# Reversed query tiles, the gated unit begun beside the last projection products, and w_out loaded in two halves

## The chip, the cores and the metric

The kernel runs on one core of a Trainium2 chip. The core's engines are TensorE (PE in the profile; PEld is its weight load), VectorE (DVE), ScalarE (ACT), GpSimd (POOL) and SyncE (SP), which issues most transfers. They run beside each other and wait for each other by semaphores. The metric is the device time of one execution in microseconds; lower is better. Before the change the median of three runs is 2513.12 us (2510.8 to 2517.88).

## The reference

One layer of a hybrid decoder over 2048 rows of width 1024, in float32 (`qa`, `ka`, `va`, `qc`, `kvc` are column blocks of `proj`, the queries and keys normed per head of 64):

```python
h = rms_norm(x, norm1_g[l])
proj = jnp.einsum('bld,de->ble', h, w_in[l])
o_a = swa_sink_mixer(qa, ka, va, sinks[l], rel_bias[:, :SWA_HEADS])
o_b = s5_mixer(proj[..., OFF_U:OFF_QC], ssm_a_re[l], ..., glu_w[l], glu_b[l])
gc = jax.nn.sigmoid(proj[..., OFF_GC:IN_WIDTH].reshape(Bsz, L, NSA_HEADS, NSA_BRANCHES))
o_c = nsa_mixer(qc, kvc, gc, cmp_pos[l], ..., rel_bias[:, SWA_HEADS:])
mixed = jnp.concatenate([rms_norm(o_a, ...), rms_norm(o_b, ...), rms_norm(o_c, ...)], axis=-1)
x = x + jnp.einsum('ble,ed->bld', mixed, w_out[l])
h2 = rms_norm(x, norm2_g[l])
hid = jax.nn.relu(jnp.einsum('bld,df->blf', h2, w_up[l]))
x = x + jnp.einsum('blf,fd->bld', hid * hid, w_down[l])
```

`swa_sink_mixer` is attention in a window of 128 with 4 query heads on 2 key heads, a learned sink per head and a bias by distance. `s5_mixer` is a complex diagonal state-space scan, then a GELU and a gated linear unit: `ab = z @ glu_w + glu_b`, the first half times the sigmoid of the second. `nsa_mixer` has 4 heads and three branches (compressed blocks, selected blocks, a window of 512), added with the 12 gates `gc` of a row. In both attentions the bias of a score depends on the distance between query and key alone:

```python
lg = jnp.where(valid, lg + bias, NEG_INF)          # bias = bias_tbl[rel_bucket(i - j + 128)]
```

## The kernel before, in words

Rows are worked in 16 tiles of 128. A float32 product is made of three matmuls (`mm3`, L76 to L78): operands are split into a high part (a cast on ACT) and a low part (a difference on DVE), and high x high, low x high and high x low are added in PSUM.

The phases, by the profile's time: `phase_front` (0 to 407 us) makes the projections in column chunks a, b, c, u, v, one product a chunk and tile, each in two half-products of 12 matmuls; beside them it computes the state-space tables and, in `ssm_steps`, the 16 pair-steps of the scan. Projections go to DRAM (`pa`, `pb`, `pc`), by stores on ACT's queue and SP's. Then (407 to about 560) the window attention (`swa_steps`), the first 11 tiles of the gated unit (`glu_steps`), the bias tables (`bias_steps`) and the block compression (`compress_steps`). `phase_mix` (to about 1240) is the sparse attention, tile by tile, with the rest of the gated unit and then the w_out products (`finish_steps`) as fillers. `phase_up` and `phase_down` are the feed-forward part.

What sets the order: `merge` interleaves lists of steps evenly by their counts, and a tile scheduler orders each engine's instructions by the written order and by priorities (the gated unit's and w_out's products have a lower one, so they fill gaps). Each engine runs its instructions in that order. SP issues its transfers in order too; they go round over eight lanes that it shares with ACT's stores, and a transfer waits for the one before it on its lane.

Three places matter here.

*The front's end.* `merge(rest[:-4], ssm_steps(...)) + rest[-4:]`: of 49 steps of the last projection chunks, 45 are merged with the state-space steps, and the last 4 half-products (L77 to L78, `pm_c`) follow alone. Then come the gated unit's first turned tile (L656, `gpt`, from `z` in SBUF), its split (L659, L660), and 13 matmuls for a half-product (`gpm`). Its weights are loaded and split by L635 to L637 (`graw`, `glu_h`, `glu_l`).

*The bias tables.* A table row per query is the same vector shifted by one. The kernel before loads it so that the partition p holds the vector from p on (`T`, 128 x 2033, for each of four heads, L736; `Ts` for the window attention), which is the table with its queries in reverse. Matmuls with the reversed identity `c_anti` (`flip`, L721) turn it over in PSUM, and ACT copies the result (L722) into `b_sel`, `b_cmp`, `b_swa`. The vector itself is made in the front by `bias_vectors` (matmul L704, copy L706, store to `r2`).

*The opening of w_out.* At tile `OPEN` = 2 of `phase_mix`, when the gated unit is done and its memory is free, `open_late` computes the norm factors of the first two mixers (`r_a`, `r_c`, by a Newton iteration of small DVE operations, L44 to L54), and `load_wout` loads the eight 128-row pieces of w_out (L1097, 512 KB each) and splits both halves of each (L1099 on ACT, L1100 on DVE). Then `finish_steps` of tile 0 turns its mixed rows (L1257, `ptx`), splits them (L1260) and makes 8 products for each half of the output columns (`pw`). The raw pieces and the residual tile `mx` share two buffers (tag "xt").

The gates of a tile are made in `prep` (tanh L1123, DVE L1124), from 12 columns that its row load brings along. Queries are turned by `turn` (L835), keys by the same.

Of the kernel before, what the change touches and what calls it, by code (L numbers as in the profile page):

```python
# [80 lines left out]
def phase_front(tc, C, x, xt_in, norm1_g, w_in, u_st, pd, rh_a, prm, dkp, dca, pre, extra, done):  # L81

    nc = tc.nc
    with ExitStack() as ctx:
# [170 lines left out]
        tp = ctx.enter_context(tc.tile_pool(name="sg", bufs=2))  # L255
# [3 lines left out]
        run(merge(rest[:-4], ssm_steps(tc, C, S, u_st, dkp, dca, tp, ps_g, ps_t)) + rest[-4:])  # L259
# [360 lines left out]
def glu_steps(tc, C, ctx, z_st, glu_w, glu_b, ob, ss, ps_x):  # L620
# [4 lines left out]
    ps = ctx.enter_context(tc.tile_pool(name="g_ps", bufs=1, space=PSUM, side="right", reuse_waits="tile"))  # L625
    wh = wp.tile([P, 4, 1024], F32R, name="glu_h")
# [65 lines left out]
def bias_vectors(tc, tp, ps, rel_bias, oh2, ohs, r2, rs):  # L692
# [5 lines left out]
    for src, dst, n in ((oh2, r2, 432), (ohs, rs, 384)):  # L698
        for j in range(src.shape[1] // n):
# [7 lines left out]
            nc.sync.dma_start(dst[:, sl], rv[:, 0:n])  # L707


def bias_steps(tc, C, B, pool, tp, ps, rel_bias, r2, rs):  # L710
# [8 lines left out]
    def flip(n, src, dst, name):  # L719
        pf = ps.tile([P, 512], F32, tag="pg", name="bpf" + name)  # L720
        nc.tensor.matmul(pf[:, 0:n], C["anti"], src, start=True, stop=True)  # L721
        nc.scalar.copy(dst, pf[:, 0:n])  # L722

    def swa(h):
        if h == 0:
            B["Ts"] = tp.tile([P, 4, 256], F32, tag="Ts", name="Ts")
            base = rs[0]
            nc.sync.dma_start(B["Ts"], bass.AP(base.tensor, base.offset, [[1, P], [384, 4], [1, 256]]))
        flip(512, B["Ts"][:, h:h + 2], B["swa"][:, h:h + 2], f"s{h}")
# [102 lines left out]
def turn(nc, C, pool, qd, h0, n, name):  # L832
    pt = pool.tile([P, 4, P], F32, tag="pt", name="pt" + name, bufs=1)
    for j in range(n):
        nc.tensor.transpose(pt[:, j], qd[:, h0 + j].rearrange("p a d -> p (a d)"), C["ident"])  # L835
# [117 lines left out]
def swa_steps(tc, C, ctx, sinks, gains, bias, pd, oa_d, ps, ss, rh):  # L953
# [14 lines left out]
    def prep(i):  # L968
# [5 lines left out]
        pt = turn(nc, C, ps_t, qd, 0, 4, f"qa{i}")  # L974
# [58 lines left out]
def phase_mix(tc, C, x, gains, B, cmp, w_out, out_norm_g, g2, pd, oa_d, ob, x1, hT, xs, rr, rh, ss_a, ss_b, r_d, rest, release):  # L1033
    nc = tc.nc
    kcA, kcB, vc = cmp
    with ExitStack() as ctx:
# [25 lines left out]
        late = {}  # L1062

        def open_late():
# [13 lines left out]
            ra, rc = (fp.tile([P, NT], F32, name=n) for n in ("r_a", "r_c"))  # L1078
            rsqrt_into(nc, sm, ra, ss_a, 1.0 / 256, NT, "ra")
# [892 lines left out]
```

## Time and profile before

| | |
|---|---|
| median of three runs | 2513.12 us |
| the profiled execution | 2511.36 us, span 2509.6 us |
| PE busy | 2428.8 us (97%) |
| DVE, ACT, POOL busy | 1754.9 us (70%), 1325.4 us (53%), 1118.8 us (45%) |
| mean granted clock of PE | 0.989 |
| flips and their copies | 14 flips on PE (28 matmuls, two for each), 14 copies on ACT |
| transfers | 328.82 MB, mean 131 GB/s |

Busy times are sums over an engine's instructions; matmuls overlap each other, so the time that a matmul adds is seen from its start to the next one's. The granted clock is a factor on PE's speed: at 0.50 the same matmuls take twice as long, and PE still shows as busy. A line of waits reads: engine, what waited, `<-` what ended the wait, then the sum, the number and the longest of the waits. A row of the windows has, after the stretch and its length, the busy time (and count) of PE, PEld, DVE, ACT and POOL, then the clock, the busy share of the DMA engines and their GB/s.

### The profile page before, as it was taken

The numbers are of one execution on the slowest core, as the hardware profiler recorded it, in microseconds if no ns is written. First come the engines' busy times: TensorE is split into PE (matmuls) and PEld (weight loads), VectorE is DVE, ScalarE is ACT, GpSimd is POOL, SyncE is SP. The second block draws the span as 40 slices with busy tenths as digits, with TensorE's granted clock in tenths as the row PEclk, the third lists the DMA queues.
The fourth block names the chain that finished last, engine by engine and source line by source line (L and its number), as shares of the span: only waits on it lengthen the run. The fifth ranks groups of instructions, "written<-read, shape, count | busy, mean of one in ns | idle before, by whom it ended". The sixth has DMA issues, their size and how long they took to land. (4 is left out here: it accounts for less than half of the span.)

```text
span 2509.6 us, 38157 instructions
## 1 busy us (share of the span) xinstructions
PE 2428.8 (97%) x12712; PEld 2051.5 (82%) x12712; DVE 1754.9 (70%) x3653; ACT 1325.4 (53%) x2767; POOL 1118.8 (45%) x1034
## 2 busy tenths in 40 slices
PE   8999999999999999999999999999999999999999
PEld 8999997787788778888788877788887888888887
DVE  4775885866688787887464455755556988888886
ACT  6354555765576665665465555555444444334442
POOL 3011222223244444454566666665654435445447
PEclk9999999999999999999999999999999999999999
DMA  5174325311221211222677666755547543444436
GB/s 178 63 211 127 114 90 170 96 56 50 67 75 47 68 47 62 79 89 81 210 213 203 190 191 186 230 163 147 149 131 261 155 124 101 135 135 127 126 100 197
DMA packets 398325, 328.82 MB, mean 131 GB/s; under 512 B 52102, under 2 KB 364044, under 8 KB 396304
## 3 DMA queue, kind: packets, MB, share of 16 engines
q1 hardware_dynamic: 360880, 299.59, 40.1%
q10 hardware_dynamic: 37248, 26.80, 3.4%
q8 instruction: 100, 1.64, 0.3%
q14 instruction: 97, 0.79, 0.1%
HBM read 213.86 MB, written 112.45 MB: 130 GB/s over the span
## 5 line engine op out<-in xcount | busy, mean ns | idle before, releaser
L1429 ACT CAST v<-vr 128x512 fp32r<-128x512 f32 x224 | 139.6, 624 | 296.0 <-DMA vr<-vd 109.1
L1429 DVE TENSOR_TENSOR v<-vr,v 128x512 fp32r<-128x512 f32 x224 | 232.2, 1044 | 78.0 <-ACT v L1429 77.7
L1767 PE MATMUL pdb<-dw,v 128*128 128x512 f32 x768 | 186.3, 392 | 2.0 <-DVE v L1429 2.0
L1767 PE MATMUL pdc<-dw,v 128*128 128x512 f32 x768 | 184.9, 389 | 2.3 <-ACT dw L1429 1.6
L1767 PE MATMUL pda<-dw,v 128*128 128x512 f32 x768 | 184.5, 389 | 0.0
L1545 POOL TENSOR_TENSOR fs<-ur,ur 128x512 f32<-128x512 f32 x64 | 94.1, 1471 | 181.1 <-DMA ur<-in_w_up 100.5
L1767 PEld LDWEIGHTS pdb<-dw,v 128*128 128x128 f32 x768 | 145.1, 189 | 32.5 <-DVE v L1429 2.4
L1429 DVE TENSOR_TENSOR ul<-ur,uh 128x512 fp32r<-128x512 f32 x96 | 91.1, 950 | 114.3 <-ACT uh L1429 114.3
L1767 PEld LDWEIGHTS pdc<-dw,v 128*128 128x128 f32 x768 | 144.0, 188 | 32.9 <-ACT dw L1429 2.0
L1767 PEld LDWEIGHTS pda<-dw,v 128*128 128x128 f32 x768 | 144.4, 188 | 30.1
L1429 ACT CAST uh<-fs 128x512 fp32r<-128x512 f32 x128 | 78.3, 621 | 144.3 <-PE pub L1574 57.1
L1429 DVE TENSOR_TENSOR ul<-fs,uh 128x512 fp32r<-128x512 f32 x128 | 131.6, 1031 | 32.3 <-ACT uh L1429 32.2
L896 POOL TENSOR_SCALAR sls<-sls,dens,gt 128x128 f32<-128x128 f32 (+15 forms) x64 | 80.4, 1257 | 124.5 <-DVE dens L895 91.9
L913 DVE TENSOR_TENSOR tls<-pps,ths 128x512 fp32r<-128x512 f32 (+1 forms) x144 | 93.8, 657 | 33.2 <-ACT ths L912 28.1
L912 ACT CAST ths<-pps 128x512 fp32r<-128x512 f32 (+1 forms) x144 | 79.8, 561 | 67.2 <-PE poc L920 53.4
L76 PE MATMUL pw<-wo_h,mh 128*128 128x512 f32 x256 | 109.2, 427 | 4.2 <-ACT mh L1259 2.0
L1574 PE MATMUL pub<-fh,uh 128*128 128x512 f32 x256 | 103.2, 403 | 4.0 <-DVE e L1583 4.0
L78 PE MATMUL pw<-wo_h,ml 128*128 128x512 f32 x256 | 104.6, 409 | 1.4 <-DVE ml L1260 1.4
L77 PE MATMUL pw<-wo_l,mh 128*128 128x512 f32 x256 | 105.5, 412 | 0.0
L896 POOL TENSOR_SCALAR slw<-slw,denw,gt 128x640 f32<-128x640 f32 (+4 forms) x64 | 53.2, 832 | 116.1 <-DVE denw L895 90.6
L1590 POOL TENSOR_TENSOR ev<-e,e 128x512 f32<-128x512 f32 x64 | 92.2, 1441 | 27.0 <-ACT e L1587 16.4
L1574 PE MATMUL puc<-fh,uh 128*128 128x512 f32 x256 | 100.9, 395 | 3.1 <-DVE eu L1583 3.1
(564 smaller groups left out, 7906.1 us busy)
## 6 DMA issues: line engine op xcount, KB each, us to landing
vr<-vd SPq DMA_DIRECT2D x224, 256.0 KB
ur<-in_w_up SPq DMA_DIRECT2D x128, 256.0 KB
vd<-ev SPq DMA_DIRECT2D x128, 256.0 KB
vd<-e ACTq DMA_DIRECT2D x64, 256.0 KB
dr<-in_w_down SPq DMA_DIRECT2D x32, 512.0 KB
x<-in_x SPq DMA_DIRECT2D x16, 512.0 KB
mx<-in_x SPq DMA_DIRECT2D x16, 512.0 KB
x<-mx ACTq DMA_DIRECT2D x16, 512.0 KB
```

The source lines that it names most:

```text
L76: nc.tensor.matmul(out, sh, mh, start=first, stop=False)
L77: nc.tensor.matmul(out, sh, ml, start=False, stop=False)
L78: nc.tensor.matmul(out, sl, mh, start=False, stop=last)
L896: nc.gpsimd.tensor_scalar(x, x, den[:, h:h + 1], gate, op0=ALU.mult, op1=ALU.mult)
L912: nc.scalar.copy(th[:, 0:nb], pt[:, 0:nb])
L913: nc.vector.tensor_tensor(tl[:, 0:nb], pt[:, 0:nb], th[:, 0:nb], op=ALU.subtract)
L1429: return (nc.scalar.copy(dh, src), nc.vector.tensor_tensor(dl, src, dh, op=ALU.subtract))
L1545: nc.gpsimd.tensor_tensor(t, x, y, op=op)
L1574: nc.tensor.matmul(bank[b], w[:, k], h[o][:, k], start=first and k == 0 and n == 0, stop=k == HALF - 1 and n == 2, skip_group_check=True)
L1590: nc.gpsimd.tensor_tensor(tile_("v" + o), x, y, op=op)
L1767: nc.tensor.matmul(bank[b, q], x[:, q, j], y[:, j], start=first and j == 0 and n == 0, stop=j == 1 and n == 2, skip_group_check=True)
```

## The change

1. Queries stand reversed in each tile of both attentions: `turn` of the queries uses `c_anti` in place of the identity, and where the mixed rows are turned for w_out, chunks 0, 1, 6 and 7 (window and sparse attention) are turned back the same way. The bias tables are loaded from DRAM already in that order, and `flip` with its copies is gone. For the compressed branch, which takes every 16th element, `bias_vectors` writes the vector also as `rc`, 8 x 16 x 135, five copies and five stores more.
2. The gates of all tiles come from one load, one flip, one tanh and one DVE operation (`gate_steps`).
3. The state-space steps are merged with 41 of the 49 steps; beside the last 8 half-products stand the first 13 steps of the gated unit (all weights and biases, three turned tiles, both half-products of tile 0); `open_glu` returns them.
4. `r_a` is computed at the beginning of `phase_mix`. `load_wout(k, n)` loads and splits one half of a piece; the first halves stand where the loads stood, the second ones between the products of tile 0's first half.

```diff
+LAST = 8
+GLU_AHEAD = 13
...
-        run(merge(rest[:-4], ssm_steps(tc, C, S, u_st, dkp, dca, tp, ps_g, ps_t)) + rest[-4:])
+        run(merge(rest[:-LAST], ssm_steps(tc, C, S, u_st, dkp, dca, tp, ps_g, ps_t)))
+        c_s.close()
+        run(merge(rest[-LAST:], open_glu()))
...
             nc.scalar.copy(rv[:, 0:n], pr[0:8, 0:n])
             nc.sync.dma_start(dst[:, sl], rv[:, 0:n])
+            if dst is r2:
+                rd = tp.tile([8, 16, 27], F32, tag="b_rd", name=f"brd{j}")
+                nc.scalar.copy(rd, pr[0:8, 0:n].rearrange("p (c r) -> p r c", r=16))
+                nc.sync.dma_start(rc[:, :, 27 * j:27 * j + 27], rd)
...
-    def flip(n, src, dst, name):
-        pf = ps.tile([P, 512], F32, tag="pg", name="bpf" + name)
-        nc.tensor.matmul(pf[:, 0:n], C["anti"], src, start=True, stop=True)
-        nc.scalar.copy(dst, pf[:, 0:n])
...
-        T = tp.tile([P, 2033], F32, tag="T", name=f"T{h}")
         base = r2[4 + h]
-        nc.sync.dma_start(T, bass.AP(base.tensor, base.offset, [[1, P], [1, 2033]]))
-        for j in range(2):
-            flip(512, T[:, 993 + 512 * j:993 + 512 * j + 512], B["sel"][:, h, 512 * j:512 * j + 512], f"{h}{j}")
-        flip(P, T[:, 0:2033:16], B["cmp"][:, h], f"c{h}")
+        nc.sync.dma_start(B["sel"][:, h], bass.AP(base.tensor, base.offset + 993, [[1, P], [1, 1024]]))
+        base = rc[4 + h]
+        nc.sync.dma_start(B["cmp"][:, h], bass.AP(base.tensor, base.offset, [[1, 8], [135, 16], [1, P]]))
...
+def gate_steps(tc, C, gt, tp, ps, src):
...
+        nc.sync.dma_start(box["g"], src.rearrange("(i p) c -> p i c", p=P)[:, :, 384:396])
...
+        nc.tensor.matmul(pf, C["anti"], box["g"].rearrange("p i c -> p (i c)"), start=True, stop=True)
+        nc.scalar.activation(flat, pf, AF.Tanh, scale=0.5)
+        nc.vector.tensor_scalar(flat, flat, 0.5, 0.5, op0=ALU.mult, op1=ALU.add)
...
-        nc.tensor.transpose(pt[:, j], qd[:, h0 + j].rearrange("p a d -> p (a d)"), C["ident"])
+        nc.tensor.transpose(pt[:, j], qd[:, h0 + j].rearrange("p a d -> p (a d)"), C[order])
...
-        def load_wout(k):
+        def load_wout(k, n):
             fp, wh, wl, go = (late[n] for n in ("fp", "wh", "wl", "go"))
-            for n in range(2):
...
+            sl = slice(512 * n, 512 * n + 512)
+            raw = fp.tile([P, D], F32, tag="xt", name=f"oraw{k}_{n}", bufs=2)[:, 0:512]
+            nc.sync.dma_start(raw, w_out[0, k * P:(k + 1) * P, sl])
+            nc.scalar.activation(wh[k][:, sl], raw, AF.Copy, scale=go[:, k:k + 1])
+            nc.vector.scalar_tensor_tensor(wl[k][:, sl], raw, go[:, k:k + 1], wh[k][:, sl], op0=ALU.mult, op1=ALU.subtract)
...
-                    nc.tensor.transpose(pt[:, j], box["mix"][:, k * P:(k + 1) * P], C["ident"])
+                    nc.tensor.transpose(pt[:, j], box["mix"][:, k * P:(k + 1) * P], C["ident" if 2 <= k < 6 else "anti"])
...
-            res = [load, lambda: turned(0, 4), lambda: turned(4, 8)] + [lambda n=n, k=k: filler(n, k) for n, k in order]
+            res = [load, lambda: turned(0, 4), lambda: turned(4, 8)] + [lambda n=n, k=k: ((load_wout(k, 1) if i == 0 and n == 0 else None), filler(n, k)) for n, k in order]
...
-                    queue += [lambda k=k: load_wout(k) for k in range(NK)]
+                    queue += [lambda k=k: load_wout(k, 0) for k in range(NK)]
...
-            run(merge(swa, glu[:cut], b_nsa + c_steps + [lambda: None] * 6))
+            run(merge(swa, glu[GLU_AHEAD:cut], b_nsa + gs[:1] + c_steps[:6] + gs[1:] + c_steps[6:] + [lambda: None] * 4))
```

What this moves on PE at the front's end. Before, the last projection matmul (`pm_c`) is followed by the gated unit's first turned tile, the flips and its first half-product (`gpm`), and the first query tile (`ptqa`):

```order
L77 MATMUL pm_c_4812<-wl_c_7_4324,hh_2432 128x396
L78 MATMUL pm_c_4812<-wh_c_7_4323,hl_2433 128x396
L656 MATMUL gpt_5024<-c_ident,z_5022 128x128 x4
L721 MATMUL bpfs_4923<-Ts,c_anti 128x512
L656 MATMUL gpt_5412<-c_ident,z_5410 128x128 x2
L721 MATMUL bpfs_4926<-Ts,c_anti 128x512
L656 MATMUL gpt_5412<-c_ident,z_5410 128x128 x2
L721 MATMUL bpf_4998<-T_4996,c_anti 128x512
L76 MATMUL gpm_5449<-glu_h,zh_5029 128x512
```

Now the second turned tile stands before the last product (`pm_c_4928`), the first in the middle of the first of the four, and half-products follow the last one directly:

```order
L664 MATMUL gpt_4903<-c_ident,z_4901 128x128 x4
L76 MATMUL pm_c_4928<-wh_c_0_4177,hh_2448 128x396
...
L78 MATMUL pm_c_4928<-wh_c_7_4407,hl_2449 128x396
L76 MATMUL gpm_4912<-glu_h,zh_4778 128x512
L77 MATMUL gpm_4912<-glu_l,zh_4778 128x512
...
L76 MATMUL gpm_4941<-glu_h,zh_4778 128x512
L664 MATMUL gpt_4979<-c_ident,z_4977 128x128 x4
L854 MATMUL ptqa_5054<-c_anti,qda_5052 128x128 x4
```

The turned tile and its split no longer stand between the last product and the first half-product, and no flip does.

On PE after the opening, where tile 0's products (`pw`) begin; before, they begin when its rows are turned (`ptx`), ahead of the probabilities' turns `ppw` of that tile:

```order
L1257 MATMUL ptx_8467<-c_ident,mix_8409 128x128 x4
L920 MATMUL poc_8510<-tls_8808,Vs 128x256 x2
...
L76 MATMUL pw_8483<-wo_h_8103,mh_8430 128x512
L77 MATMUL pw_8483<-wo_l_8104,mh_8430 128x512
L78 MATMUL pw_8483<-wo_h_8103,ml_8431 128x512
...
L909 MATMUL ppw_8921<-c_ident,slw_8695 128x128
```

Now `ppw_8902`, the same turns, stand ahead of the second `ptx`, and two further groups of them before the first product:

```order
L928 MATMUL ppw_8902<-c_ident,slw_8676 128x128
...
L1271 MATMUL ptx_8419<-c_ident,mix_8361 128x128 x2
L1271 MATMUL ptx_8419<-c_anti,mix_8361 128x128 x2
...
L928 MATMUL ppw_9002<-c_ident,slw_8797 128x128
L76 MATMUL pw_8439<-wo_h_8091,mh_8382 128x512
```

The products of tile 0 begin later in PE's order.

On SP after the opening, where the loads of w_out stand. Before, the eighth piece (`oraw`), the residual tiles of tiles 0 and 1 (`mx`), the next tile's projections (`tc`):

```order
L1097 DMA oraw_8351<-in_w_out 128x1024
L1097 DMA oraw_8385<-in_w_out 128x1024
L1245 DMA mx_8412<-in_x 128x1024
L1245 DMA mx_8878<-in_x 128x1024
L1104 DMA tc_9815<-pb 128x256
```

Now the second halves (`oraw_1`) stand between the two residual tiles, with the next tile's projections among them:

```order
L1259 DMA mx_8364<-in_x 128x1024
L1115 DMA oraw_1_8435<-in_w_out 128x512
L1115 DMA oraw_1_8463<-in_w_out 128x512
L1115 DMA oraw_1_8480<-in_w_out 128x512
L1115 DMA oraw_1_8505<-in_w_out 128x512
L1121 DMA tc_9790<-pb 128x256
L1122 DMA tc_9790<-pc 128x256
L1115 DMA oraw_1_8557<-in_w_out 128x512
...
L1259 DMA mx_8859<-in_x 128x1024
```

The projections wait behind four of the second halves, and the residual tile of tile 1 behind all eight.

More of the change, by code (lines that the diff above doesn't have):

```diff
@@ L1030, with phase_mix @@
 LOAD_BASE = 16
-def phase_mix(tc, C, x, gains, B, cmp, w_out, out_norm_g, g2, pd, oa_d, ob, x1, hT, xs, rr, rh, ss_a, ss_b, r_d, rest, release):
+def phase_mix(tc, C, x, gains, B, cmp, w_out, out_norm_g, g2, pd, oa_d, ob, x1, hT, xs, rr, rh, ss_a, ss_b, r_d, gates, rest, release):
     nc = tc.nc
@@ L1061, in phase_mix @@
         vw = {}
-        late = {}
+        late = {"ra": kp.tile([P, NT], F32, name="r_a")}
+        rsqrt_into(nc, sm, late["ra"], ss_a, 1.0 / 256, NT, "ra")
         def open_late():
@@ L1077, in open_late @@
             nc.sync.dma_start(go, out_norm_g[0].rearrange("(k p) -> p k", p=P))
-            ra, rc = (fp.tile([P, NT], F32, name=n) for n in ("r_a", "r_c"))
-            rsqrt_into(nc, sm, ra, ss_a, 1.0 / 256, NT, "ra")
+            ra = late["ra"]
+            rc = fp.tile([P, NT], F32, name="r_c")
             rsqrt_into(nc, sm, rc, ss_b, 0.25 / 512, NT, "ra")
@@ L1121, in prep @@
             split_v(nc, vw[i], tcc[:, 448:512])
[L1122 to L1125 removed]
+            return qA, qB, gates[:, i].rearrange("p (h b) -> p h b", b=3)
         def cmp_steps(i, qA, qB, gt, po):
@@ L1866, in trunk @@
         rs = dr.tile([8, 384], F32, name="rs")
+        rc = dr.tile([8, 16, 135], F32, name="rc")
         r_d = dr.tile([L], F32, name="r_d")
@@ L1873, in trunk, with open_glu, beside @@
         pre = c_pre.enter_context(tc.tile_pool(name="pre", bufs=1, side="right"))
+        c_g = c_all.enter_context(ExitStack())
+        G_ = {}
+        def open_glu():
+            def beside():
+                G_["ps"] = c_g.enter_context(tc.tile_pool(name="x_pg", bufs=1, space=PSUM, side="right", reuse_waits="tile"))
+                return G_["ps"]
+            G_["steps"] = glu_steps(tc, C, c_u, u_st, glu_w, glu_b, ob, ss_b, beside)
+            return G_["steps"][:GLU_AHEAD]
         phase_front(tc, C, x, x_t, norm1_g, w_in, u_st, pd, rh_a, (a_re, a_im, log_dt, b_re, b_im, c_re, c_im, d_skip), dkp, dca,
-                    pre, late_loads, c_pre.close)
+                    pre, late_loads, c_pre.close, open_glu)
         c_b = c_all.enter_context(ExitStack())
@@ L1878, in trunk @@
         B = {}
-        with ExitStack() as c_g:
+        with c_g:
             def pool(name, bufs, **kw):
@@ L1882, in trunk @@
             ps_a = [pool(f"x_p{n}", bufs, space=PSUM) for n, bufs in (("q", 2), ("p", 2), ("o", 1), ("t", 1))]
-            ps_x = pool("x_pg", 1, space=PSUM)
+            ps_x, glu = G_["ps"], G_["steps"]
             xs = pool("x_s", 1)
-            C["anti"] = xs.tile([P, P], F32, name="c_anti")
+            C["anti"] = bp.tile([P, P], F32, name="c_anti")
             nc.sync.dma_start(C["anti"], k_anti)
@@ L1897, in trunk @@
             cut = len(glu) - 3 * (T16 - GLU_BESIDE) + 1
-            run(merge(swa, glu[:cut], b_nsa + c_steps + [lambda: None] * 6))
-        phase_mix(tc, C, x, gains, B, cmp, w_out, out_norm_g, norm2_g, pd, oa_d, ob, x1, hT, sums, rr, rh_c, ss_a, ss_b, r_d, glu[cut:], c_u.close)
+            gs = gate_steps(tc, C, gates, xs, ps_x, pd["c"])
+            run(merge(swa, glu[GLU_AHEAD:cut], b_nsa + gs[:1] + c_steps[:6] + gs[1:] + c_steps[6:] + [lambda: None] * 4))
+        phase_mix(tc, C, x, gains, B, cmp, w_out, out_norm_g, norm2_g, pd, oa_d, ob, x1, hT, sums, rr, rh_c, ss_a, ss_b, r_d, gates, glu[cut:], c_u.close)
         c_b.close()
```

68 lines of the change are left out of this document (32 added, 36 removed).

## The prediction

> **What bounds the kernel now.** I read the page's busy table first, then its chain of waits, then the table of windows, which shows where TensorE (PE) loses time.
>
> ```profile
> span 2509.6 us, 38157 instructions
> PE 2428.8 (97%) x12712; PEld 2051.5 (82%) x12712; DVE 1754.9 (70%) x3653; ACT 1325.4 (53%) x2767; POOL 1118.8 (45%) x1034
> PE 35%; issue 1%; DVE 1%; DMA 0%; POOL 0%; ACT 0%; SPq 0%; DVEq 0%; POOLq 0%; ACTq 0%
> core 0: 2509.6 us, clock 0.989
> ```
>
> PE is busy 2428.8 of 2509.6 us and heads the chain. So 80.8 us of PE idle is all that waiting costs, and a mean clock of 0.989 costs about 28 us more (0.011 x 2509.6). A saving must be PE work that disappears, PE idle that closes, or a stretch of lowered clock that goes away. The windows (PE, PEld, DVE, ACT and POOL busy, then the granted clock, the DMA share and GB/s) at the three places that the change touches, from the front's end through the sliding-window part to the opening of w_out:
>
> ```profile
> 240.00:380.00 140.00, 139.24 (x872) 134.61 (x872) 122.89 (x267) 74.37 (x158) 32.89 (x28) 1.00 0.37 109
> 380.00:400.00 20.00, 20.00 (x119) 19.34 (x118) 6.36 (x18) 8.96 (x19) 4.95 (x6) 1.00 0.30 85
> 405.00:430.00 25.00, 21.33 (x100) 14.40 (x98) 14.24 (x43) 16.71 (x46) 7.93 (x7) 0.93 0.83 235
> 420.00:425.00 5.00, 4.65 (x20) 3.19 (x19) 2.70 (x11) 3.66 (x10) 1.69 (x2) 0.66 0.66 204
> 430.00:460.00 30.00, 24.07 (x140) 17.21 (x140) 27.11 (x83) 23.36 (x74) 6.84 (x7) 1.00 0.52 140
> 675.00:685.00 10.00, 6.03 (x35) 4.52 (x35) 9.98 (x53) 7.35 (x19) 3.10 (x5) 0.97 0.59 199
> 685.00:700.00 15.00, 13.40 (x55) 10.98 (x55) 13.63 (x41) 10.95 (x25) 6.84 (x7) 0.57 0.55 175
> 700.00:727.00 27.00, 25.55 (x170) 21.71 (x168) 23.86 (x88) 20.64 (x54) 9.62 (x13) 1.00 0.19 64
> 727.00:755.00 28.00, 27.17 (x193) 24.24 (x192) 24.32 (x82) 19.98 (x53) 14.04 (x22) 1.00 0.11 35
> ```
>
> To be seen: while the state-space steps run beside the last projections (240 to 400) PE is full. From 405 to 430 it idles 3.67 us, and the clock of 0.66 in 420 to 425 costs 1.7 (0.34 x 5). From 430 to 460 it idles 5.93 us with VectorE (DVE) at 90%. From 675 to 700 DVE is busy 23.61 of 25 us, PE idles 5.57 and the clock costs 6.7 (0.43 x 15 and 0.03 x 10). The bias flips, the transfers and the w_out splits behind this:
>
> ```profile
> 408.88 0.41 PE L656 MATMUL gpt<-c_ident,z 128*128 128x128 f32 x2 [0.68 <-DVE zl L660]
> 411.35 1.10 PE L721 MATMUL bpf<-T,c_anti 128*128 128x512 f32 x2 [0.97 <-ACT zh L659]
> 406.44 0.53 SPq L970 DMA_DIRECT2D ta<-pa  x1
> 412.21 0.32 SPq L971 DMA_DIRECT2D ta<-pb  x1
> PE pqw L885 <- DVE nmc L888: 3.4, 2, 2.3
> 680.66 2.80 DVE L1100 SCALAR_TENSOR_TENSOR wo_l<-oraw,wo_g,wo_h 128x512 fp32r<-128x512 f32 x4
> ```
>
> At the front's end PE waits for the first tiles of the gated unit to be split on ACT and DVE (0.68, 0.97). SP's queue stands still from 406.44 to 412.21, and with it the second query tile and what is queued behind. At 680 the scores wait 2.3 us while DVE makes four splits of w_out in a row (2.80 us).
>
> **The flips.** Ten flips of 512 columns and four of 128 leave PE.
>
> ```profile
> 426.38 1.02 PE L721 MATMUL bpf<-T,c_anti 128*128 128x512 f32 x2
> 426.84 0.68 PE L886 MATMUL pqa<-wa,qBa 128*128 128x256 f32 x1
> 428.40 0.60 PE L721 MATMUL bpfc<-T,c_anti 128*128 128x128 f32 x2
> 428.64 0.47 PE L920 MATMUL poa<-tha,va 128*128 128x256 f32 x1
> 445.22 1.12 PE L721 MATMUL bpf<-T,c_anti 128*128 128x512 f32 x2
> 446.19 0.38 PE L835 MATMUL ptka<-c_ident,qda 128*128 128x128 f32 x2
> 407.00:451.00 44.00, 6.92 (x14) 0.96 0.74 214
> ```
>
> From a flip's start to the next instruction's it is 0.46 to 0.97 us for 512 columns and 0.24 for 128. Ten and four are 5.6 to 10.7 us. On ACT 14 copies go, 6.92 us (the last row, ACT alone). Since DVE is at 90% in 430 to 460, part of what PE no longer does there comes back as waiting: three quarters of the upper figure would be 8.0, and half 5.3; I take -6.5, with bounds of -10.7 and -3 (only the flips up to 430 count, where DVE is at 57%: five of 512 and one of 128 are about 3). Turning the queries with the other constant costs what it cost. The bias tables still come from DRAM, 4 x 0.5 MB and four small loads in place of four of 1 MB, so the queue is lighter, not heavier.
>
> **The gated unit's beginning beside the last four products.** Its eight weight loads, the splits, the first three turned tiles and two half-products are placed among the last eight half-products. Their costs beside a product:
>
> ```profile
> 399.02 0.34 PE L78 MATMUL pm_c<-wh_c,hl 128*128 128x396 f32 x1
> 406.57 0.34 PE L78 MATMUL pm_c<-wh_c,hl 128*128 128x396 f32 x1
> L636 ACT CAST glu_h<-graw x8: 607/618/631, 398.8 to 439.3; 128x512 fp32r<-128x512 f32 x8
> L637 DVE TENSOR_TENSOR glu_l<-graw,glu_h x8: 675/692/1823, 399.5 to 439.9; 128x512 fp32r<-128x512 f32 x8
> ```
>
> 42 matmuls from 399.02 to 406.57 are 0.18 us each, so a half-product of 12 is 2.16 us and the last eight are 17.3 us. The eight splits are 5.5 us of DVE and 4.9 of ACT, against 6.36 and 8.96 busy in the 20 us of 380 to 400, so both fit. The matmuls moved ahead cost what they cost later. What the move takes away is the waits at 408.88 and 411.35 and those up to 430: -3.7, and the lowered clock with them, -1.7. Something may be left while the first query tile is loaded, doubled on POOL and turned, so I take -5, with bounds of -5.4 and 0 (the waits come again at the first query tile). The 5.93 us of 430 to 460 are DVE's ramp of the window attention; one split of weights (0.69) per few us less and fewer ACT copies help it, fewer gated-unit products to fill it hurt it. I take 0, bounds -5.9 (all closed) and +3 (half as much again).
>
> **The state-space steps squeezed.** They are merged with 41 half-products where there were 45, so 8.6 us of PE cover (4 x 2.16) leave them. DVE has 129.3 us of work in the 160 of 240 to 400 (81%) and now must do it in about 151 (86%). The nearest row for a stretch in which DVE is nearly full is
>
> ```profile
> 300.00:320.00 20.00, 19.26 (x124) 18.43 (x123) 19.01 (x48) 9.31 (x22) 4.90 (x4) 1.00 0.35 92
> ```
>
> 0.74 us of PE idle per 20 us at 95%. Seven such stretches would cost 5.2 us, none 0; I take +1, since 86% is nearer to the 88% of 240 to 380, where PE idles 0.76 us in all.
>
> **The w_out split.** At the opening, 8 splits of 0.744 us and the r_a chain (some ten small operations like the one shown, 0.16 us each from start to end and about 0.1 from start to start) leave DVE:
>
> ```profile
> L1100 DVE SCALAR_TENSOR_TENSOR wo_l<-oraw,wo_g,wo_h x16: 740/744/1200, 680.7 to 704.7; 128x512 fp32r<-128x512 f32 x16
> 677.42 0.16 DVE L54 TENSOR_TENSOR r_a<-r_a,rat 128x16 f32<-128x16 f32 x1
> L1099 ACT ACTIVATE wo_h<-oraw,wo_g x16: 705/712/732, 679.4 to 702.8; 128x512 fp32r<-128x512 f32 x16
> ```
>
> That is 6.0 + 1.0 = 7.0 of its 23.6 us, so 16.6 are left for a stretch in which PE has 12.7 us of work at full clock (6.03 + 13.40 - 6.7). DVE would still set its length, so it shortens by about 7.0. Two things come back. The first products of tile 0 move behind this stretch (the order on PE): six matmuls at about 0.23 us (a pass of 512 columns, half of the flip at 426.38) and eight narrower ones at 0.12 are +2.4 in 700 to 727, where PE is nearly full. And the second halves' splits, 6.0 us, land in 700 to 755, where DVE is busy 48.2 of 55. It has room for 6.8, but its order fixes that some scores wait: +2, a third of the splits. The sum is -2.6; I take -3. The bounds are -12.3 (idle and clock loss both gone) and +6 (nothing gained here, each late split on the path). In this stretch PE would still idle a quarter of the time, so I leave the lowered clock where it is.
>
> [...]
>
> **The small parts.** One tanh and one DVE operation replace 16 of each, the front gains five copies on ACT:
>
> ```profile
> L1123 ACT ACTIVATE gt<-tc x16: 197/208/295, 576.3 to 1043.9; 128x12 f32<-128x12 f32 x16
> L1124 DVE TENSOR_SCALAR gt<-gt x16: 153/165/484, 578.7 to 1044.8; 128x12 f32<-128x12 f32 x16
> L706 ACT COPY brv<-bpr x6: 469/502/512, 54.2 to 72.2; 8x432 f32<-8x432 f32 x5, 8x384 f32<-8x384 f32 x1
> 50.00:60.00 10.00, 9.72 (x49) 7.73 (x48) 4.87 (x10) 6.12 (x13) 0.00 (x0) 1.00 0.73 206
> ```
>
> 2.6 us of DVE and 3.3 of ACT leave, spread over 470 us; at PE's side about 0. The five copies are 2.5 us of ACT, which is busy 6.12 of 10 there while PE loses 0.28. The product that follows waits at most one copy more: +0.5, bounds 0 and +2.5 (every copy on PE's path). The new store's rows of 108 bytes go through the same queue. [...] The bias tables are read some 350 us after it, the gates from 576 on.
>
> **Sum.** -6.5 - 5 + 0 + 1 - 3 + 0.5 = -13.0 us against the profiled execution's 2511.36: 2498.4. The median of the three runs, 2513.12, is 1.8 above that execution, so I predict 2500.
>
> **The rivals.** A measurement of this kernel can tell about 0.3% (7.5 us) from no change, so a median under 2505.6 is faster and one over 2520.6 slower.
>
> 1. *The sliding-window stretch is bound by DVE, and PE only waits where it flipped.* For: DVE 27.11 of 30 in 430 to 460. Against: PE is busy 97.51 of 100 from 460 to 560, so flips' time saved is only lost in the first 50 us. Flips -3, the transition -1.7 (clock alone), w_out 0, squeeze +1, small +0.5: -3, about 2510. This is also where it comes out if the first query tile is late: SP's wait of 5.8 us for an earlier store is repeated before it.
>
> 2. *The opening is healed.* The clock stays at 1.00 from 675 to 700, and the ramp closes by two thirds. For: DVE's work there falls from 23.6 to 16.6 us. Against: nothing fills PE there, now less than before. w_out -9 in place of -3 and the ramp -4: -23, about 2490.
>
> 3. *Slower: the second halves choke tile 0's products.* They go through the two buffers that the residual tile shares, so that in effect one is free: a load waits for the split before it, and the next tile's projections stand behind it in SP's queue. For: the order on SP puts that tile's load between the fourth and the fifth half. Against: eight loads have 55 us, 6.9 us each, while cast and split are 1.46. It decides once DVE's share of 700 to 755 (88%) comes to that of 675 to 700 (94%): the 6.0 us added would make it 98%. Then 25 us there cost what they cost at the opening, 12.3, and twice that in 55 us: 24.6, and the opening gains nothing (+3): -13 + 3 + 24.6 = +14.6, about 2528.
>
> **How the numbers follow.** The forecast has 0.52, rival 1 0.24, rival 2 0.16, rival 3 0.08. [...] Lowered clocks at places that nothing here touches (585 to 595) may fall otherwise:
>
> ```profile
> 585.00:590.00 5.00, 5.00 (x22) 4.17 (x22) 3.21 (x16) 2.92 (x12) 1.92 (x5) 0.54 0.20 55
> 590.00:595.00 5.00, 5.00 (x19) 4.38 (x19) 3.34 (x17) 2.98 (x13) 2.74 (x6) 0.50 0.00 0
> ```
>
> 4.8 us are lost in these two rows, so the forecast's own case reaches 5 us to both sides, 2495 to 2506. The range reaches to rival 2 and past rival 1: 2488 to 2513, which leaves out the slower case and a little at the lower end. Faster: the forecast but for its upper edge, and rival 2, 0.50 + 0.16 and 0.02 of rival 1: 0.68. Slower: 0.07. The rest, 0.25, is within 0.3%.
>
> **What would show it.** Right: PE at 100% from the last projection product through the first two gated half-products, and no clock under 1 in the 25 us after; no wait named for a bias table; the 25 us after w_out's opening done in 18 to 20; the first tile's products with their second halves never named as a wait. Wrong: PE idle beside DVE at over 90% in the window attention's first 40 us (rival 1), clock 0.5 in the two tiles after the opening (rival 3), or PE idle of more than 2 us among the state-space steps (the squeeze was mis-sized).

## The result and the profile after

The changed kernel takes 2490.67 us (median; 2512.51 for the kernel before beside it): a ratio of 0.9911, 95% interval 0.9891 to 0.9931. One of its four timings, 2938.41 us at a granted clock of 0.752, is of a slow execution, and the ratio leaves it out. The forecast was 2500 us, between 2488 and 2513, and faster; the change is 21.8 us where 13 were worked out.

The page's busy rows and the cores' row after:

```profile
span 2489.3 us, 38153 instructions
PE 2415.2 (97%) x12686; PEld 2043.9 (82%) x12686; DVE 1762.6 (71%) x3638; ACT 1318.0 (53%) x2743; POOL 1117.4 (45%) x1034
core 0: 2489.3 us, clock 0.992
```

PE idles 74.1 us where it idled 80.8. Adding (1 - clock) x length over windows of 5 us gives 20.4 us lost to the lowered clock where it was 26.7. So of the 20.3 us that the span is shorter, 6.7 are waiting, 6.3 are clock, and 7.3 are PE work that is gone (PE work is here the span less idle and less lost clock). The windows that answer to those shown of before, at the same places in the program (the columns are as there):

```profile
240.00:390.00 150.00, 147.26 (x918) 140.97 (x917) 126.75 (x276) 78.86 (x168) 36.47 (x32) 1.00 0.37 109
410.00:430.00 20.00, 17.17 (x95) 13.12 (x95) 13.77 (x44) 12.81 (x39) 5.37 (x5) 1.00 0.84 230
430.00:460.00 30.00, 27.83 (x178) 22.68 (x177) 27.38 (x86) 22.42 (x75) 9.85 (x10) 1.00 0.45 114
655.00:665.00 10.00, 7.08 (x48) 6.12 (x47) 9.67 (x48) 7.08 (x21) 3.08 (x4) 0.93 0.61 160
665.00:680.00 15.00, 14.04 (x72) 11.54 (x70) 12.24 (x36) 11.06 (x25) 5.56 (x6) 0.70 0.36 108
680.00:707.00 27.00, 25.07 (x163) 21.07 (x164) 25.09 (x86) 20.37 (x53) 10.82 (x15) 1.00 0.25 82
1220.00:1235.00 15.00, 9.86 (x35) 7.61 (x34) 13.93 (x12) 7.93 (x11) 10.19 (x12) 0.77 0.42 143
```

Beside the state-space steps PE now idles 2.74 us (it was 0.76 from 240 to 380). Where the window attention begins, it idles 2.83 and 2.17 instead of 3.67 and 5.93, at full clock. At w_out's opening (655 to 680) it idles 3.88 and loses 5.2 to the clock, instead of 5.57 and 6.7. The last row shows 5.1 us of idle and 3.4 of clock where the feed-forward part begins. The waits by name, from the front, the opening and that last place (engine, what waited, what ended the wait, sum, number, longest):

```profile
PE pv L586 <- ACT BT L571: 2.7, 4, 1.3
PE pqc L904 <- DVE nmw L907: 2.6, 1, 2.6
PE pud L1588 <- DVE fl L1443: 5.1, 1, 5.1
```

The kernel before has a loss of the same kind, 4.6 us of idle and 3.4 of clock, but just ahead of its last w_out product (at 1249.4 us), and spread over several waits:

```profile
1220.00:1235.00 15.00, 11.69 (x53) 8.81 (x51) 9.59 (x20) 7.45 (x16) 12.32 (x21) 0.96 0.71 226
1235.00:1250.00 15.00, 13.70 (x50) 10.68 (x51) 6.44 (x7) 5.42 (x6) 7.31 (x7) 0.81 0.68 234
```

To see where the span went I cut both executions at the same marks on PE: the last projection matmul, the first turned query (`ptqc`) of the sparse attention's tiles 0, 3, 8 and 15, the last w_out matmul, the first matmul of `phase_down`. Each stage's length is followed by what of it is PE idle + lost clock (summed over windows of 2.5 us):

| stage | before | after | difference |
|---|---|---|---|
| front | 406.6 (12.4 + 1.7) | 409.6 (14.4 + 0) | +3.0 |
| window attention | 169.8 (13.5 + 1.7) | 156.9 (9.4 + 0) | -12.9 |
| tiles 0 to 3 | 50.6 (2.5 + 5.1) | 44.0 (1.9 + 6.8) | -6.6 |
| tiles 3 to 8, with the opening | 159.2 (10.7 + 8.5) | 154.8 (8.1 + 5.1) | -4.4 |
| tiles 8 to 15 | 319.1 (18.2 + 0) | 315.5 (12.6 + 1.7) | -3.6 |
| to the last w_out product | 144.0 (7.5 + 3.4) | 140.0 (5.6 + 0) | -4.0 |
| feed-forward, up | 639.3 (7.1 + 3.4) | 646.7 (13.0 + 5.1) | +7.4 |
| feed-forward, down | 620.9 (8.9 + 3.0) | 621.8 (8.9 + 1.7) | +0.9 |

One execution's stage is good to some 4 us where transfers and clock come into it: the front's instructions are the same in the kernel before and in one of the experiments (the gates alone), and took 406.6 and 410.7. Two neighbours have to be read together. Tiles 0 to 3 are shorter by PE work that is done elsewhere, 35.3 us for 43.0; their idle and lost clock are 8.7 for 7.6. And a stall lies behind the last w_out product that lay ahead of it before: from tile 15 to `phase_down` it is 786.7 us for 783.3, 3.4 more.

### The profile page after: what moved, and what is told of

Same layout as the page of the kernel before. It is cut to its first block, busy times and chain, and to the rows that moved or that the text cites. A ratio compares the mean times of both kernels' runs of the same rounds, so it can differ in the third digit from the quotient of the medians.

```text
span 2489.3 us, 38153 instructions
## 1 busy us (share of the span) xinstructions
PE 2415.2 (97%) x12686; PEld 2043.9 (82%) x12686; DVE 1762.6 (71%) x3638; ACT 1318.0 (53%) x2743; POOL 1117.4 (45%) x1034
## 4 chain that ended last, share of the span: by engine, by line
PE 66%; DVE 6%; DMA 2%; issue 2%; ACT 2%; POOL 1%; SPq 0%; DVEq 0%; ACTq 0%; POOLq 0%
PE pub L1588 7%; PE puc L1588 7%; PE pdb L1781 7%; PE pdc L1781 7%; PE pda L1781 7%; PE pua L1588 7%; PE pud L1588 3%; PE pdd L1781 3%; PE poc L939 3%; PE pw L76 2%; PE pw L78 2%; PE pw L77 2%; PE pps L928 2%; PE pqs L904 1%; PE pqs L905 1%
## 5 line engine op out<-in xcount | busy, mean ns | idle before, releaser
L1443 DVE TENSOR_TENSOR v<-vr,v 128x512 fp32r<-128x512 f32 x224 | 240.4, 1080 | 73.1 <-ACT v L1443 73.0
L915 POOL TENSOR_SCALAR sls<-sls,dens,gates 128x128 f32<-128x128 f32 (+15 forms) x64 | 80.2, 1253 | 124.4 <-DVE dens L914 95.9
L928 PE MATMUL pps<-c_ident,sls 128*128 128x128 f32 x544 | 101.4, 276 | 2.6 <-POOL sls L915 1.3
```

The lines of the kernel that those rows point to most:

```text
L915: nc.gpsimd.tensor_scalar(x, x, den[:, h:h + 1], gate, op0=ALU.mult, op1=ALU.mult)
L928: nc.tensor.transpose(pt[:, j, hh], sls[hh][:, (b0 + j) * P:(b0 + j + 1) * P], C["ident"])
L1443: return (nc.scalar.copy(dh, src), nc.vector.tensor_tensor(dl, src, dh, op=ALU.subtract))
```

## The experiments

The changed kernel has three parts that can be had apart: the reversal with the gates (without flips, the gates need the reversed order of one load), the early beginning of the gated unit, and w_out's halves. Four kernels took one alone or one away.

Each experiment was timed beside the kernel before, whose median was 2509.86 to 2511.22 us there and 2512.51 beside the changed kernel, so ratios compare better than microseconds. Five variants of the changed kernel that came out near it (ratios 0.9924 to 0.9933, their intervals overlapping its own) suggest that its own 0.9911 is a little lucky: 17 to 22 us is what the change is worth. The profiled execution is one of an experiment's timings and not its median; for w_out's halves alone, the early beginning taken away and the gates taken away it is the longest of them (2516.17, 2502.85 and 2500.92 us).

**The reversal and the gates alone**

```diff
-LAST = 8
-GLU_AHEAD = 13
+LAST = 4
+GLU_AHEAD = 0
...
-        def load_wout(k, n):
+        def load_wout(k):
...
+            for n in range(2):
+                sl = slice(512 * n, 512 * n + 512)
+                if n == 0:
+                    raw_k = fp.tile([P, D], F32, tag="xt", name=f"oraw{k}", bufs=2)
+                    nc.sync.dma_start(raw_k, w_out[0, k * P:(k + 1) * P])
```

(taken from the changed kernel, with `r_a` back in `open_late`)

> The kernel before with the reversed queries and the one-piece gates alone: no flips, no early beginning of the gated unit, both halves of w_out at the opening. Theory (flips are PE work that nothing gives back): 7.3 us of PE work go and the clock loss of 1.7 us at 420 to 425 with them, so about 2504 against 2512.5. Rival (the window attention there is bound by DVE, so PE waits where it flipped): about 2510, with PE idle from 407 to 460 growing from 9.6 us to 14 or more.

Measured: 2496.7 us beside 2510.44, ratio 0.9952 (0.9934 to 0.997). That is more than either theory gave, and the profile shows that the stages move in opposite ways. PE's work (span less idle less lost clock) falls from 2402.1 to 2394.8, by 7.3. But the window attention is hardly shorter, 167.8 us for 169.8, though 9.8 us of PE work left it: its idle is 16.2 for 13.5 and its lost clock 6.8 for 1.7. Its first 25 us:

```profile
403.00:428.00 25.00, 18.18 (x81) 14.60 (x80) 15.26 (x47) 13.89 (x42) 7.08 (x6) 0.73 0.71 192
PE ptqa L854 <- POOL qda L847: 1.7, 1, 1.7
PE gpt L664 <- DVE zl L668: 1.5, 1, 1.5
PE gpm L76 <- DVE zl L668: 1.4, 1, 1.4
```

6.82 us of idle where it was 3.67, and a clock of 0.73. Of the rival the mechanism is there, at the gated unit's first tiles and the first query tile and not where DVE is full (in the next 30 us the idle is 2.72, for 5.93). Over these 55 us the idle is 9.5, as before, and not the 14 that the rival named; what grew is the lost clock. The next stage gives more than half of it back: tiles 0 to 3 are 4.0 us shorter, with no lowered clock. From the last projection product to tile 3 this kernel takes 214.5 us for 220.5, 6.0 less, where 9.0 us of PE work are gone; so a third came back as waiting, which is less than one execution's noise. Tiles 3 to 8 gain 4.2 more, 8 to 15 4.0.

**w_out's halves and the early r_a alone**

```diff
 (the kernel before)
-        def load_wout(k):
+        def load_wout(k, n):
...
-                    queue += [lambda k=k: load_wout(k) for k in range(NK)]
+                    queue += [lambda k=k: load_wout(k, 0) for k in range(NK)]
```

> The kernel before with w_out's halves apart and r_a early alone. Theory (the opening is bound by DVE, and 7 us less of it there shorten it): 4 to 8 us less, about 2506. Rival (the second halves cost later what the opening saves, and the lowered clock stays): 2511 to 2514, no change.

Measured: ratio 1.0 (0.9989 to 1.0012). No change, as the rival said. The opening itself is shorter by what the prediction worked out, though more by the clock than by the idle:

```profile
672.00:682.00 10.00, 7.09 (x46) 5.75 (x45) 9.56 (x49) 7.41 (x21) 3.40 (x5) 0.98 0.53 131
682.00:697.00 15.00, 14.09 (x81) 11.75 (x81) 14.10 (x39) 11.25 (x25) 7.14 (x10) 0.90 0.48 147
```

Idle 3.8 for 5.57 and clock 1.7 for 6.7. From tile 3 to tile 4 it is 27.9 us for 35.8, and from 4 to 5 32.7 for 37.4; the next two tiles are 30.3 and 30.0 for 26.8 and 26.0. So 12.6 us were gained and 7.5 given back at once. In this execution what was left went in tiles 8 to 15 (+2.8, of it 3.4 clock), up to the last product (+1.7) and where the feed-forward part begins (+5.7).

**The early beginning taken away**

```diff
-LAST = 8
-GLU_AHEAD = 13
+LAST = 4
+GLU_AHEAD = 0
```

> The changed kernel with the gated unit's beginning put back behind the last product (4 half-products alone, nothing ahead). Theory (the wait for the first turned tiles costs 3.7 us and the squeeze of the state-space steps 2): 2 to 5 us more, about 2494 against 2490.7. Rival (the early beginning only moves the wait into the state-space steps): within 1 us of 2490.7.

Measured: 2497.18, ratio 0.9949 (0.9932 to 0.9967) against 0.9911. The early beginning is worth some 6.5 us by the medians (2497.2 less 2490.7) and 9.5 by the ratios; the intervals touch and do not overlap. In the profile the window attention is 166.8 us (idle 16.4, clock 5.1) against 156.9 (9.4, 0), and the front 404.7 against 409.6. So 9.9 less 4.9 there, and 7.4 up to tile 3 (617.9 us against 610.4).

**w_out's halves taken away**

```diff
-                    queue += [lambda k=k: load_wout(k, 0) for k in range(NK)]
+                    queue += [lambda k=k: load_wout(k) for k in range(NK)]
...
-            res = [load, lambda: turned(0, 4), lambda: turned(4, 8)] + [lambda n=n, k=k: ((load_wout(k, 1) if i == 0 and n == 0 else None), filler(n, k)) for n, k in order]
+            res = [load, lambda: turned(0, 4), lambda: turned(4, 8)] + [lambda n=n, k=k: filler(n, k) for n, k in order]
```

> The changed kernel with both halves of w_out at the opening again and r_a late. Theory (opening bound by DVE): 4 to 8 us more, about 2497 against 2490.7. Rival (no net effect of the split; the tiles after it went faster by an accident of lowered clocks): 2490 to 2492.

Measured: 2490.89, ratio 0.9924 (0.9908 to 0.994). By the medians the rival: no net effect. By the ratios it is 3.3 us with intervals that overlap, so a small gain isn't excluded. Tiles 3 to 8 take 154.9 us with both halves at the opening and 154.8 with them apart; the opening's longest wait is 3.4 us (`pqc` behind DVE) for 2.6, and tile 0's first product comes 25.9 us after the last of the gated unit's for 25.6.

The tiles 8 to 15 took 314.0 to 315.5 us in the four kernels so far with the reversal and the gates, and 319.1 and 321.9 without. Nothing of the flips or of w_out stands there. What does is the gates.

**The gates alone, and the gates taken away**

```diff
 (the kernel before, gates of all tiles at once, not reversed)
-            gt = small(12, "gt")
-            nc.scalar.activation(gt, tcc[:, 512:524], AF.Tanh, scale=0.5)
-            nc.vector.tensor_scalar(gt, gt, 0.5, 0.5, op0=ALU.mult, op1=ALU.add)
-            return qA, qB, gt.rearrange("p (h b) -> p h b", b=3)
+            return qA, qB, gates[:, i].rearrange("p (h b) -> p h b", b=3)
...
```

> The kernel before with the gates of all tiles made at once (one load of 16 x 12 per partition, one tanh, one DVE operation; rows in their old order, so no flip of it) and nothing else. Theory (the five to seven us that the sparse attention's tiles gained in every kernel with the reversal come from the gates, whose tanh and DVE step stand in each tile's queue): 4 to 8 us less than the kernel before, about 2505, with PE idle from the first w_out product to the last query tile falling from 21.6 to 16. Rival (they come from the flips and the order of the queries): no change, 2510 to 2513.

```diff
 (the changed kernel)
-        nc.scalar.activation(flat, pf, AF.Tanh, scale=0.5)
-        nc.vector.tensor_scalar(flat, flat, 0.5, 0.5, op0=ALU.mult, op1=ALU.add)
+        nc.scalar.copy(flat, pf)
...
-            return qA, qB, gates[:, i].rearrange("p (h b) -> p h b", b=3)
+            gt = small(12, "gt")
+            nc.scalar.activation(gt, gates[:, i], AF.Tanh, scale=0.5)
+            nc.vector.tensor_scalar(gt, gt, 0.5, 0.5, op0=ALU.mult, op1=ALU.add)
+            return qA, qB, gt.rearrange("p (h b) -> p h b", b=3)
```

> The changed kernel with the gates' tanh and DVE step back in each tile (the flipped raw columns are kept from one load). Theory (gates): 4 to 8 us more, about 2496 against 2490.7, PE idle in the tiles after w_out's opening back at 21. Rival: 2490 to 2492.

Measured: the gates alone 2512.24, ratio 1.0006 (0.9993 to 1.0018); the gates taken away 2496.89, 0.9941 (0.992 to 0.9962). By the whole time the first is the rival's, no gain at all, and the second the theory's. The tiles 8 to 15, one row for each kernel (before, after, the gates alone, the gates taken away), show that in this stage the theory holds:

```profile
786.29:1105.36 319.07, 300.87 (x1920) 255.99 (x1919) 250.23 (x799) 197.59 (x473) 139.68 (x203) 1.00 0.21 65
```

```profile
765.21:1080.76 315.55, 302.98 (x1924) 257.68 (x1924) 248.38 (x796) 196.29 (x468) 139.27 (x204) 0.99 0.20 66
```

```profile
787.95:1102.24 314.29, 301.74 (x1923) 256.33 (x1923) 248.39 (x796) 195.93 (x468) 139.11 (x204) 1.00 0.21 66
```

```profile
766.38:1086.70 320.32, 302.22 (x1920) 257.28 (x1919) 251.48 (x799) 197.59 (x473) 139.15 (x203) 0.99 0.21 65
```

PE idles 18.2, 12.6, 12.6 and 18.1 us: 5.6 go with the gates in both pairs, with 1.8 to 3.1 us of DVE. All traces agree: 12.1 to 13.4 us of idle in the ten kernels whose gates are made at once, 18.1 to 18.3 in the three that make them in each tile. But the two small operations are not all that differs. The tile scheduler writes another order: of some 1918 PE instructions in these tiles over 500 stand at another place, on DVE 166 of 792. The three kernels with gates in each tile share one order, and nine of the ten others share a second one. So the cause lies with the gates' change; whether it is the two operations or the order that came with them, no run tells.

In the kernel with the gates alone the profiled execution lost it again between tile 15 and the last product, where its order is its own and it took 151.1 us for 144.0:

```profile
PE pw L76 <- ACT mh L1272: 4.6, 1, 4.6
PE poc L936 <- ACT thw L928: 2.8, 1, 2.8
```

**The flips put back**

```diff
 (the changed kernel; results not used)
+    def flip(n, src, name):
+        pf = ps.tile([P, 512], F32, tag="pg", name="bpf" + name)
+        nc.tensor.matmul(pf[:, 0:n], C["anti"], src, start=True, stop=True)
+        dst = tp.tile([P, 512], F32, tag="b_scr", name="bsc" + name)
+        nc.scalar.copy(dst[:, 0:n], pf[:, 0:n])
...
+        for j in range(2):
+            flip(512, B["sel"][:, h, 512 * j:512 * j + 512], f"{h}{j}")
+        flip(P, B["cmp"][:, h], f"c{h}")
```

> The changed kernel with 14 flips and 14 copies put back on PE and ACT, their results unused. Theory (flips are PE work, 7.3 us, with nothing to hide in): 6 to 9 us more, about 2498 against 2490.7. Rival (the window attention waits for DVE, and the flips fit into its waits): 0 to 3 us more.

Measured: 2499.88, ratio 0.9954 (0.9939 to 0.9969): 9 us more, the theory's. PE's work is 2404.8 us (2499.8 less 78.5 idle and 16.5 clock) against 2394.8, 10.0 more, and most of it lies in the window attention, 170.3 us for 156.9, of which idle 12.0 for 9.4. So with the early beginning in place the flips have nothing to hide in; without it (the first experiment) about a third of what they cost came back up to tile 3.

**Buffers of their own for the second halves**

```diff
-            raw = fp.tile([P, D], F32, tag="xt", name=f"oraw{k}_{n}", bufs=2)[:, 0:512]
+            raw = fp.tile([P, D if n == 0 else 512], F32, tag="xt" if n == 0 else "xw", name=f"oraw{k}_{n}", bufs=2)[:, 0:512]
```

> The changed kernel with two buffers of their own for the second halves of w_out, so that they no longer share with the residual tiles. Theory (the shared buffers don't delay a product: no wait of a product for a second half): within 2 us of 2490.7. Rival (they choke tile 0's products, which hides the gain of the split): 3 to 6 us less, about 2486.

Measured: 2493.02, ratio 0.993 (0.9911 to 0.9948). No gain: sharing the buffers costs nothing that can be seen. (To make room, `r_b` overwrites `r_c`.)

**The opening spread thinner**

```diff
-                    queue += [lambda k=k: load_wout(k, 0) for k in range(NK)]
+                    queue += [lambda k=k: load_wout(k, 0) for k in range(HEAD)]
...
+        def more_wout(n, k):
+            if n == 0 and k + HEAD < NK:
+                load_wout(k + HEAD, 0)
+            elif n == 0:
+                load_wout(2 * (k + HEAD - NK), 1)
+                load_wout(2 * (k + HEAD - NK) + 1, 1)
+            elif k + 2 * HEAD < NK:
+                load_wout(k + 2 * HEAD, 1)
```

(HEAD = 2; called before each product of tile 0)

> The changed kernel with only two first halves of w_out split at its opening; the other six stand between tile 0's products of the first half, the second halves between the later products. Theory (the splits in a row at the opening cost idle and lowered clock, and would cost less if spread; but what is saved there is given back in the next two tiles, where DVE is as full): tiles 3 to 8 take 152 to 156 us as in all kernels so far, 2488 to 2493. Rival (the opening's idle and clock loss, 8 us in the changed kernel, go): 147 to 149 us for these tiles, about 2484.

Measured: 2491.76, ratio 0.9933 (0.9913 to 0.9953), tiles 3 to 8 157.1 us (idle 7.9, no lowered clock). The rival came true in half: the clock loss of 5.1 went. The time didn't: these tiles hold 149.2 us of PE work for 141.5, since products that others make later are made here, the stages after it are 5.6 us shorter, and the feed-forward part begins with 3.7 more.

**The state-space steps squeezed harder**

```diff
-LAST = 8
+LAST = 12
```

> The changed kernel with 12 half-products left for the gated unit's beginning, the state-space steps merged with 37. Theory (each half-product of 2.16 us taken from them costs idle when DVE is the bound there, as 1 us of the four taken did): 4 to 8 us more idle before the last projection product, 2494 to 2500. Rival (the idle in the front is the same in all kernels and moves with the transfers): within 2 us of 2490.7.

Measured: 2491.57, ratio 0.9928 (0.9909 to 0.9946). The time is the rival's, the wait is the theory's. PE's wait for these steps, with 45, 41 and 37 half-products beside them (before, after, this kernel):

```profile
PE pv L579 <- ACT BT L564: 0.7, 1, 0.7
```

```profile
PE pv L586 <- ACT BT L571: 2.7, 4, 1.3
```

```profile
PE pv L586 <- ACT BT L571: 6.7, 7, 2.0
```

2.0 us for the first four taken and 4.0 for the next four. The front is 413.6 us for 409.6; what made up for it is spread over the later stages within their noise, and the interval would hold 4 us either way.

**The order where the feed-forward part begins**

```diff
-            if k == 0:
+            if k == 1:
                 W["u"] = weights(0, 0)
```

> The changed kernel with the first weights of the feed-forward part split after its two first input factors, not between them. Theory (the 5.1 us for which PE waits there, and the lowered clock behind it, come from the second factor's split standing in DVE's queue behind five splits of weights that run beside POOL at 1.7 us instead of 0.7): the wait shrinks to under 2 us, 4 to 7 us less, about 2485 against 2490.7. Rival (the transfers of 1200 to 1245, which keep the DMA engines full, bring the factors so late that DVE's order is idle): the wait stays, 2490 to 2493.

Measured: 2491.58, ratio 0.9929 (0.9912 to 0.9946). The wait named in the result went, and others took its place:

```profile
PE pub L1588 <- ACT fh L1443: 4.1, 1, 4.1
PE puc L1588 <- DVE fl L1443: 2.3, 1, 2.3
```

The stage took 649.1 us for 646.7. So the order of these splits is not what holds it back. All kernels but two took 645 to 653 us there, for 639.3; those two (the kernel before and the gates alone) have a stall just ahead of it. With the stretch from tile 15 to the last product counted in, every kernel is slower than the kernel before, by 1.6 to 11.1 us. That is measured; why, isn't settled. The factors come over DRAM from the last tiles' rows (`hT`, then `sums`), the DMA engines are full just ahead (share 1.05 from 1205 to 1220 in the changed kernel), and DVE is busy 13.93 of the next 15 us; no run here tells these apart.

## Why the prediction was right, and where it was not

Direction and range were right, and 13 us were too few. In whole times the reversal with the gates is worth about 12 us and the early beginning 6.5 to 9.5 on top; the split of w_out shows nothing. Step by step:

- **The flips**, -6.5 between 3 and 10.7. Mis-sized: PE's work fell by 7.3 (first experiment) and rose by 10.0 when they were put back. The upper row, 0.97 us to the next instruction, was as near as the lower one. "Part of what PE no longer does there comes back as waiting" holds for the first experiment: 2 of 9.8 us are kept in the window attention, and 6.0 of 9.0 up to tile 3. It doesn't hold for the whole change, where all of it counts.
- **The early beginning**, -5 and 0 for the ramp. Measured in the window attention, idle and clock: -4.1 and -1.7 against the kernel before; -7.0 and -5.1 against the kernel without it. The sum came near, but not for the reason given, and that is luck. The waits up to 430, priced at -3.7, hardly moved: 3.67 us before, 2.83 after, again at the gated unit's split and the first query tile. The ramp from 430 to 460, set to 0, fell from 5.93 to 2.17; in the first experiment, without the early beginning, it had already fallen to 2.72. The two stand in for each other in the sum. Without flips and without the early beginning the first stretch is worse than before (6.82 us, clock 0.73), so there the early beginning has more to remove. No run takes the early beginning alone with the flips in place and nothing else changed.
- **The squeeze**, +1 between 0 and 5.2. It was +2.0, named as waits for ACT's copy `BT`, while DVE was busy 126.75 of 150. The sign that the prediction set for this, more than 2 us of idle among these steps, did show: 2.74.
- **The w_out split**, -3. Measured 0 when it is made alone, and 0 to 3.3 us when it is taken away. The step "it shortens by about 7.0" was right in size (7.9 to tile 4 in the kernel that has it alone) and in part by luck: 5.0 of it is lowered clock, which the step left where it was, and 1.8 is idle. "+2, a third of the splits" was too little for what comes back: 7.5 us in the next two tiles. DVE is busy 47.0 of the 52 us from 655 to 707, so I read it as the bound there, with the order of its splits moving time from tile to tile; the bound itself was not tested.
- **The small parts**, "at PE's side about 0". This step failed. With 16 pairs of small operations gone, 5.9 us of ACT and DVE in sum, PE idles 5.6 us less in tiles 8 to 15 alone, and the whole kernel gains 6.2 us by the medians (7.5 by the ratios, though the intervals overlap); added alone to the kernel before it gains nothing. I counted their busy time and not that the scheduler would write another order without them. Which of the two it is stays open.
- **Nothing for the end of the attention.** The stall at the feed-forward part's beginning was in no term and no rival. The kernel before has one too, just ahead of the mark; over both stages the loss is 3.4 us here and 1.6 to 11.1 in the other kernels.
- **The clock.** "I leave the lowered clock where it is" at the opening: it is 5.2 for 6.7. By stages it moved by up to 3.4 us either way and fell by 6.3 in sum; the forecast had 1.7 of it. The rest may be luck: it comes in pieces of 1.7 us, and the five variants near this kernel lost 15.4 to 18.8 us in all, for 20.4 here.

Rival 1's mechanism showed in the first experiment, in one stage above all, and not in the whole change. Rival 2's time, 2490, is the measured one, and of its two reasons one came true: the ramp closed by two thirds (5.93 to 2.17), and the opening was not healed (5.2 us of clock for 6.7). Rival 3 is refuted by the time, and the buffers of their own show no cost of sharing them.

## What to carry to other kernels

Cut the profiles at marks of the program, stage by stage, with idle and lost clock apart: the kernel before and the one with the gates alone, equal in time, differed here by 4 to 7 us in three stages. Then add neighbouring stages before calling a gain lost or a loss new, since waits, lowered clock and filler work move across a mark: of what the first experiment lost again in the window attention, more than half was back by tile 3, and the feed-forward part's stall had stood just ahead of the mark. And where a scheduler orders the program, compare the orders first: removing sixteen pairs of small operations also moved hundreds of others.

## What the runs showed of the hardware

The clock is lost in equal pieces. A single dip is a 5 us window at 0.66 or 0.67, 1.7 us, and the stages of the kernel before and of the changed one lost 1.7, 3.4, 5.1, 6.8 or 8.5 us, near enough (the last stage, which ends with the execution, aside): 3.4 us at half clock, once to five times over. The row that shows one piece, of the kernel before:

```profile
140.00:145.00 5.00, 4.09 (x22) 4.09 (x23) 1.77 (x4) 2.42 (x6) 0.00 (x0) 0.67 0.76 170
```

The clock falls without PE idling for as long as such a piece lasts: at w_out's opening the longest waits ahead of the fall are 2.3 us before and 2.6 after, in 10 us of which PE is busy 6.03 and 7.08.

In the traces of these two kernels every change of the clock lies on a grid of 3413 ns, with 3.41, 6.83, 10.24 or 13.65 us at half clock in a stretch (what lies at the end of the execution aside), and whether it falls goes with how much PE is busy in one piece of that grid. Over the two traces, from 20 us after the start, the clock fell after 8 of the 8 pieces at full clock in which PE was busy under 1.5 us, after 4 of 13 with 1.5 to 1.9, after 3 of 56 with 1.9 to 2.8, and after none of 1346 above that. The two pieces ahead of the fall at w_out's opening in the kernel before, and the four at half clock behind it:

```profile
677.54:680.95 3.41, 2.38 (x15) 1.80 (x15) 3.41 (x21) 2.05 (x6) 1.74 (x3) 1.00 0.65 232
680.95:684.37 3.42, 1.17 (x9) 0.88 (x7) 3.42 (x10) 2.75 (x7) 0.63 (x1) 1.00 0.35 121
684.37:698.02 13.65, 12.05 (x44) 9.80 (x43) 12.26 (x33) 10.44 (x22) 5.32 (x7) 0.50 0.54 169
```

So a wait of about 2 us can cost lowered clock on top if it falls inside one piece of the grid, as the 2.25 us from 681.45 to 683.70 did here: four pieces followed, 6.8 us.

DVE's splits can run slowly beside POOL. Where the feed-forward part begins, of the changed kernel:

```profile
1217.29 5.19 DVE L1443 TENSOR_TENSOR ul<-fs,uh 128x512 fp32r<-128x512 f32 x3
1225.78 0.68 DVE L1443 TENSOR_TENSOR ul<-fs,uh 128x512 fp32r<-128x512 f32 x1
1220.30 1.64 POOL L1559 TENSOR_TENSOR fs<-fs,ur 128x512 f32<-128x512 f32 x1
1223.60 1.71 POOL L1559 TENSOR_TENSOR fs<-ur,fs 128x512 f32<-128x512 f32 x1
```

The same split takes 1.73 us while POOL adds the weights and 0.68 when POOL's last addition is done at 1225.3. Over the changed kernel it took 0.68 or 0.69 us in all 80 cases with POOL idle, and 0.68 to 1.84 in the other 144, beside POOL for a part of the time or all of it. POOL can be the one that pays: its addition takes 1.28 to 1.30 us alone and up to 3.34 beside DVE.
